# Attention scores on row halves inside column blocks, and a pair's probabilities side by side

## The chip, the cores and the metric

The kernel runs on one core of one Trainium2 chip. The metric is device time in microseconds for one execution of the whole program, lower is better. All numbers are fp32 in the inputs and the output.

## The reference

Two layers of an encoder trunk over 256 tokens of width 1024. Each layer is a SwiGLU half-step, a mixer, a second SwiGLU half-step and a gated input of a per-layer embedding. The change lies in the mixer, of which this is the outline:

```python
u = rmsnorm(x, g_mix[i]) @ w_in[i]                 # (256, 3072)
q, k, v, hy = jnp.split(u, [512, 1024, 1536], axis=-1)
y_na = neighbourhood_attention(q, k, v, na_rpb[i]) # 8 heads of 64
...                                                # short convolution of hy, split into x0, x1, hv
y_hy = x0 * long_conv(hv * x1, filt, hy_bias[i])   # 512 channels
y = jnp.concatenate([_rms(y_na), _rms(y_hy)], axis=-1) * g_out[i]
x = x + y @ w_out[i]
```

The attention's neighbourhood is a mask of the full 256 x 256 scores: per head s = q k^T / 8 + bias (a very negative number outside the neighbourhood), softmax over the keys, then the product with v.

## The kernel before

Activations are kept transposed: 128 channels on the partitions, 256 tokens along the free dimension. Matrix products are done in fp32r with every operand split in two parts, h (rounded) and l (the rest), and three products h·h, h·l, l·h; `mm3` is that. ScalarE makes h by a copy, VectorE makes l by a subtraction. Weights stream from HBM in pieces of 16 tiles on SP's queue and are split by ScalarE (L283) and VectorE (L285) in the same way.

The program is written as one order of matmuls, with everything else in "fibers", Python generators that issue a few instructions and then yield. A tick lets every live fiber take one step. `paced` counts the products that have been issued in units of 256 columns of an `mm3` and ticks once every three units, nine narrow matmuls. `fb.finish()` steps a fiber to its end, so that what it makes has been issued before the matmul that reads it. TensorE and ScalarE run in the order written; for the other engines the order is the framework's scheduler's. There are 8 PSUM banks, handed out by `bank()`, each 128 x 512 fp32.

The mixer runs through the list `ORDER`, token by token. `g0` to `g3`, `q0` to `q3`, `x0`, `x1` are column blocks: two products of 8 weight tiles each with the normed input, 48 narrow matmuls into the two halves of one bank (`columns`). A q block makes the queries and the keys of one pair of heads (128 channels: 64 of the even head, 64 of the odd one); class `QK` scales them by the norm (L728), and splits them: the keys whole (L733, L737), the queries into a zeroed tile of twice the width in which each head's 64 rows stand in a half of the columns of its own (L735, L739). `s` is the score block of a pair: for each head, two products of 128 queries with 256 keys, on all 128 rows, where the other head's rows are the zeros. `softmax` then works on one bank of a head: L762 and L764 on VectorE, L769 on ScalarE, a reciprocal L772, L776. `t` transposes the probabilities of a pair, 128 x 128 at a time (L783), one bank for each head, and splits them (L792, L794). `p` is `attend`: for each head and each half of the keys one `mm3` of v's 128 columns (the head's own 64 and 64 zeros) with that head's transposed probabilities, so that one 128 x 256 result holds both heads. `values` makes these zero-padded tiles of v: four memsets for each half of the tokens on POOL (L696, L697), a scaling L701, and copies and subtractions by quarters (L708, L712). `head_norm` scales the result (L802, L805) and adds up its squares, from which `Rstd` makes the norm of the attention's output: matmuls with ones (L415), a chain on VectorE (L388 to L432), a spread to all rows (L439).

`u` and `f` are the transposes and the forward transform of the long convolution, `i` its way back, `a` the projection of the attention's output, after which the other output's projection follows. The weights on the host are laid out in the order of the column blocks.

Of the kernel before, what the change touches and what calls it, by code (L numbers as in the profile page):

```python
# [79 lines left out]
def hybrid_trunk(ctx: ExitStack, tc: tile.TileContext, w, xT, pT, rpb, small, wf, zT, dft, idft, decay, out):  # L80
# [583 lines left out]
    def mixer(i):  # L664
# [25 lines left out]
        vh = [[t2(F32R, "vh") for _ in range(2)] for _ in range(2)]  # L690
        vl = [[t2(F32R, "vl") for _ in range(2)] for _ in range(2)]

        def values():
            for tt in range(2):
                for pp in range(2):
                    G.memset(f(vh[tt][pp]), 0.0)  # L696
                    G.memset(f(vl[tt][pp]), 0.0)  # L697
            yield from rs.wait()
            for tt in range(2):
                vf = t2()  # L700
                V.tensor_scalar(vf, vps[tt], rs.r[:, tt : tt + 1], None, op0=ALU.mult)  # L701
                yield
                for pp in range(2):
                    src = vf[:, pp * 256 : (pp + 1) * 256].rearrange("p (a b c) -> p a b c", a=2, b=2)
                    hv, lv = v2(vh[tt][pp]), v2(vl[tt][pp])
                    for par in range(2):
                        cs = slice(par * 192, par * 192 + 64)
                        S.copy(hv[:, :, cs], src[:, :, par])  # L708
                    yield
                    for par in range(2):  # L710
                        cs = slice(par * 192, par * 192 + 64)
                        V.tensor_sub(lv[:, :, cs], src[:, :, par], f(hv[:, :, cs]))  # L712

        class QK:


            def __init__(self, b):
                self.kh, self.kl = t1(F32R), t1(F32R)
                self.qh, self.ql = t2(F32R), t2(F32R)
                self.fb = spawn(self.go(b))  # L720

            def go(self, b):
                G.memset(f(self.qh), 0.0)
                G.memset(f(self.ql), 0.0)
                yield from rest(EV)
                yield from rs.wait()
                q = t2()
                V.tensor_tensor(v2(q), v2(b), rb2(), op=ALU.mult)  # L728
                yield
                where = [  # L730
                    (slice(64 * par, 64 * par + 64), slice(T * par, T * par + T)) for par in range(2)
                ]
                S.copy(self.kh, q[:, T:])  # L733
                for r, c in where:
                    S.copy(self.qh[r, c], q[r, :T])  # L735
                yield
                V.tensor_sub(self.kl, q[:, T:], f(self.kh))  # L737
                for r, c in where:
                    V.tensor_sub(self.ql[r, c], q[r, :T], f(self.qh[r, c]))  # L739

        class Head:
# [7 lines left out]
            def scores(self, st):  # L749
                st.fb.finish()  # L750
                b = bank()
                for tt in range(2):
                    qs = slice(T * self.par + tt * P, T * self.par + (tt + 1) * P)
                    mm3(b[:, tt * T : (tt + 1) * T], st.qh[:, qs], st.ql[:, qs], st.kh, st.kl, True, True)
                self.e = t2()
                self.fb = spawn(self.softmax(b), True)
# [21 lines left out]
            def turn(self):  # L778
                self.fb.finish()
                b = bank()  # L780
                for kt in range(2):
                    for tt in range(2):
                        PE.transpose(  # L783
                            b[:, kt * T + tt * P : kt * T + (tt + 1) * P],
                            self.e[:, tt * T + kt * P : tt * T + (kt + 1) * P],
                            ident,
                        )
                self.h, self.l = t2(F32R), t2(F32R)
                self.fb = spawn(self.parts(b), True)

            def parts(self, b):
                S.copy(self.h, b)  # L792
                yield
                V.tensor_sub(self.l, b, f(self.h))  # L794

# [11 lines left out]
        def attend(pair, hs):  # L807
            vfb.finish()
            ps = bank()[:, :T]
            n = 0  # L810
            for h in hs:
                h.fb.finish()
                for kt in range(2):
                    cs = slice((pair % 2) * 256 + h.par * P, (pair % 2) * 256 + (h.par + 1) * P)
                    ks = slice(kt * T, (kt + 1) * T)
                    a, b = vh[kt][pair // 2][:, cs], vl[kt][pair // 2][:, cs]
                    mm3(ps, a, b, h.h[:, ks], h.l[:, ks], n == 0, n == 3)
                    n += 1
            hl = t2(F32R, "y")
            yna.append((hl, spawn(head_norm(ps, nsq, pair, hl))))  # L820
# [41 lines left out]
        def turn(hs):  # L862
            for h in hs:
                h.turn()

        def scores(pair, st):
            hs = [Head(pair, par) for par in range(2)]
            for h in hs:
                h.scores(st)
            return hs  # L870
# [64 lines left out]
        def add(c, ps, st, e):  # L935
# [4 lines left out]
            e.tensor_add(x[c], x[c], t)  # L940
# [21 lines left out]
        qs, hs, added, wo = {}, {}, [], Tiles()  # L962
        for kind, j in MIXER:
            if kind == "g":
                gated(j, columns())
            elif kind == "q":
                qs[j] = QK(columns())
            elif kind == "x":
                outer(2 * j, columns())
            elif kind == "s":  # L970
                hs[j] = scores(j, qs.pop(j))
            elif kind == "t":
                turn(hs[j])
            elif kind == "p":
                attend(j, hs.pop(j))
                if len(yna) == 4:
                    na = Rstd(rna, nsq.parts, HY, [fb for _, fb in yna], STAT_NA, SPREAD_NA)
            elif kind == "u":
                u_turned()
            elif kind == "f":  # L980
                forward(j)
            elif kind == "i":
                backward(j)
                if len(yhy) == 4:
                    hy = Rstd(rhy, hsq.parts, HY, [fb for _, fb in yhy], STAT_HY, SPREAD_HY)
            elif kind == "a":
                added.append(spawn(add(j, project(wo, j, yna), na, V)))
        wo = Tiles()
        new_norm()
        for c in range(KD):  # L990
            ps = project(wo, c, yhy)

            def both(c=c, ps=ps):
                added[c].finish()
                yield from add(c, ps, hy, V)
# [165 lines left out]
def _weights(a):  # L1161
# [16 lines left out]
    for i in range(DEPTH):  # L1178
# [3 lines left out]
        for kind, j in MIXER:  # L1182
# [71 lines left out]
```

## Time and profile before

| | |
|---|---|
| time, median of 3 runs | 1093.13 us (1092.15 to 1093.78) |
| the profiled execution's own time | 1093.29 us |
| its span, first to last instruction | 1091.5 us |
| granted TensorE clock, mean | 0.994 |
| busy: PE, weight load, DVE, ACT, POOL | 1064.5, 964.0, 912.1, 649.4, 196.2 us |

PE is TensorE's matmuls, DVE VectorE, ACT ScalarE, POOL GpSimd; L12 is a line of the kernel. A matmul's duration runs to the modelled end of its result, so neighbouring matmuls overlap and a busy share near 100% doesn't by itself say how dense they are; the distance between two starts does. The mixers lie at about 213 to 329 us and 743 to 860 us of the span.

### The profile page before, as it was taken

To read this page: it belongs to the slowest core of one execution; us is meant where nothing else is said; L and a number is where in the kernel's file an instruction comes from. 1 tells how busy PE (TensorE), PEld (TensorE's weight loads), DVE (VectorE), ACT (ScalarE), POOL (GpSimd) and SP (SyncE) were. 2 spreads that over 40 slices of the span, in tenths; PEclk is the share of its full clock that TensorE was granted. 3 is DMA by queue.
4 is the path that set the end of the run, shared out by engine and by line. 5 is a ranking of instruction groups with operands and counts; after the bars stand their busy time and mean duration, and the time that the engine had idled before them with its cause. 6 is when DMAs were issued, how large, how long until landed. Compare 5 with 4: busy or idle time off the path is not lost.

```text
span 1091.5 us, 17975 instructions
## 1 busy us (share of the span) xinstructions
PE 1064.5 (98%) x6716; PEld 964.0 (88%) x6716; DVE 912.1 (84%) x1590; ACT 649.4 (59%) x1182; POOL 196.2 (18%) x232
## 2 busy tenths in 40 slices
PE   7989999999999999999999999999999999999995
PEld 6878888899997888888988888889999888888895
DVE  4999987898999988766789999788889999886564
ACT  7566665376736766544666665635765566665443
POOL 3111120411212211100111113023131311110101
PEclk9999999999999999999999999999999999999998
DMA  9566545554425655555465654555513465555621
GB/s 325 192 202 231 193 160 188 192 195 151 139 97 184 210 194 187 187 188 191 157 219 180 231 194 158 190 171 180 195 73 117 140 217 198 191 190 177 209 78 39
DMA packets 32983, 194.07 MB, mean 178 GB/s; under 512 B 3584, under 2 KB 6528, under 8 KB 10880
## 3 DMA queue, kind: packets, MB, share of 16 engines
q1 hardware_dynamic: 32896, 192.92, 51.6%
q8 instruction: 53, 0.87, 0.3%
q14 instruction: 34, 0.28, 0.1%
HBM read 191.86 MB, written 1.05 MB: 177 GB/s over the span
## 4 chain that ended last, share of the span: by engine, by line
PE 85%; DVE 10%; DMA 2%; ACT 2%; issue 1%; SPq 0%; ACTq 0%; DVEq 0%
PE ps L190 40%; PE ps L199 21%; PE ps L169 7%; PE ps L170 7%; PE ps L171 7%; DVE wl L285 3%; DMA raw<-in_w 2%; DVE x L940 1%; DVE s L939 1%; DVE rt L396 1%; DVE xg L367 1%; ACT wh L283 1%; PE ps L783 1%; DVE y L805 0%; PE ps L415 0%
## 5 line engine op out<-in xcount | busy, mean ns | idle before, releaser
L285 DVE TENSOR_TENSOR wl<-raw,wh 128x1024 fp32r<-128x1024 f32 (+1 forms) x350 | 427.6, 1244 | 98.4 <-PE ps L199 62.1
L283 ACT CAST wh<-raw 128x1024 fp32r<-128x1024 f32 (+1 forms) x350 | 362.1, 1041 | 156.8 <-PE ps L190 82.7
L190 PE MATMUL ps<-xg,wh 128*128 128x512 f32 x1408 | 346.7, 395 | 10.6 <-DVE xg L1088 6.5
L190 PEld LDWEIGHTS ps<-xg,wh 128*128 128x128 f32 x1408 | 259.3, 190 | 62.7 <-DVE xg L1088 7.2
L199 PEld LDWEIGHTS ps<-xg,wl 128*128 128x128 f32 x1408 | 182.4, 192 | 7.7
L199 PE MATMUL ps<-xg,wl 128*128 128x256 f32 x1408 | 184.6, 283 | 0.0
L190 PE MATMUL ps<-act,wh 128*128 128x512 f32 x704 | 173.0, 391 | 0.0
L190 PEld LDWEIGHTS ps<-act,wh 128*128 128x128 f32 x704 | 128.3, 189 | 23.8
L487 POOL TENSOR_TENSOR gu<-gu,rb 128x256 f32<-128x256 f32 x88 | 69.3, 792 | 393.1 <-DVE gu L207 324.6
L169 PE MATMUL ps<-xg,wh 128*128 128x256 f32 x448 | 127.5, 285 | 0.0
L171 PE MATMUL ps<-xg,wl 128*128 128x256 f32 x448 | 126.8, 283 | 0.0
L170 PE MATMUL ps<-xg,wh 128*128 128x256 f32 x448 | 126.7, 283 | 0.0
L353 POOL TENSOR_TENSOR acc<-acc,q 128x256 f32<-128x256 f32 x62 | 56.1, 905 | 328.9 <-ACT q L350 327.7
L199 PEld LDWEIGHTS ps<-act,wl 128*128 128x128 f32 x704 | 92.9, 191 | 5.1
L199 PE MATMUL ps<-act,wl 128*128 128x256 f32 x704 | 94.4, 282 | 0.0
L170 PEld LDWEIGHTS ps<-xg,wh 128*128 128x128 f32 x448 | 86.0, 192 | 0.1
L169 PEld LDWEIGHTS ps<-xg,wh 128*128 128x128 f32 x448 | 85.9, 192 | 0.1
L171 PEld LDWEIGHTS ps<-xg,wl 128*128 128x128 f32 x448 | 85.9, 192 | 0.0
L204 ACT COPY gu<-ps 128x256 f32<-128x256 f32 x176 | 56.1, 373 | 31.5 <-PE ps L199 31.2
L207 DVE TENSOR_TENSOR gu<-gu,ps 128x256 f32<-128x256 f32 x176 | 66.1, 411 | 0.0
L365 ACT ACTIVATE xg<-x,sm 128x256 fp32r<-128x256 f32 x56 | 28.1, 507 | 57.8 <-DVE x L524 40.4
L494 DVE TENSOR_TENSOR s<-s,gu 128x256 f32<-128x256 f32 x88 | 55.0, 634 | 0.4 <-ACT s L491 0.2
(194 smaller groups left out, 1298.7 us busy)
## 6 DMA issues: line engine op xcount, KB each, us to landing
raw<-in_w SPq DMA_DIRECT2D x172, 1024.0 KB, 4.9
bias<-in_rpb SPq DMA_DIRECT2D x16, 256.0 KB, 2.7
raw<-in_w SPq DMA_DIRECT2D x4, 256.0 KB, 4.8
x<-in_xT SPq DMA_DIRECT2D x8, 128.0 KB, 4.8
raw<-in_w SPq DMA_DIRECT2D x2, 512.0 KB, 5.3
t<-in_wf SPq DMA_DIRECT2D x4, 256.0 KB, 5.7
dec<-in_decay SPq DMA_DIRECT2D x4, 256.0 KB, 5.7
out<-o SPq DMA_DIRECT2D x4, 256.0 KB, 2.5
```

The lines of the kernel that those rows point to most:

```text
L169: PE.matmul(o, lh, rh, start=start, stop=False)
L170: PE.matmul(o, lh, rl, start=False, stop=False)
L171: PE.matmul(o, ll, rh, start=False, stop=stop)
L190: PE.matmul(b, lh, r, start=start, stop=False)
L199: PE.matmul(o, ll, rh, start=False, stop=stop)
L204: S.copy(dst, b[:, T:])
L207: V.tensor_add(dst, dst, b[:, :T])
L283: S.copy(h[:, a : a + k], src)
L285: V.tensor_sub(l[:, a : a + k], src, f(h[:, a : a + k]))
L353: G.tensor_add(self.ac, self.ac, q)
L487: G.tensor_mul(u, u, rb)
L494: V.tensor_mul(s, s, u)
```

## The change

- The queries are no longer set into a zeroed tile. `QK` scales the block, copies it whole (h) and subtracts whole (l), one 128 x 512 operation each; the two memsets of each pair on POOL go.
- A score block works on 64 rows at a time: the even head's on rows 0 to 63, the odd one's on rows 64 to 127, in turn, into two banks. The count of matmuls stays 12.
- `s0`, `s1` and `s2` are issued between the two halves of a column block (`q1+s0`: after the first product of q1), and the order of the other tokens changes.
- The transposes of a pair are ordered by the half of the keys, with both heads' probabilities side by side in one bank, so that they can be the 512 columns of one product.
- `attend` multiplies v's 128 columns of the pair, unpadded, by these 512 columns: 6 wide matmuls in place of 12 narrow ones. Of the 128 x 512 result two diagonal blocks are wanted; ScalarE copies them (2 copies of 64 x 256) into a tile in SBUF, one tick ahead of `head_norm`, which now reads that tile.
- `values` is one ScalarE scaling and one VectorE multiply-subtract for each half of the tokens, straight from PSUM; its memsets go.

```diff
-ORDER = "g0 q0 g1 s0 q1 g2 t0 s1 g3 q2 t1 p0 u0 q3 f0 s2 f1 p1 s3 t2 x0 x1 t3 i0 p2 p3 i1 i2 i3 a0 a1 a2 a3 a4 a5 a6 a7"
-MIXER = [(t[0], int(t[1])) for t in ORDER.split()]
+ORDER = "g0 q0 g1 q1+s0 g2 g3 t0 q2+s1 p0 u0 q3+s2 t1 f0 f1 p1 t2 s3 x0 x1 t3 i0 p2 p3 i1 i2 i3 a0 a1 a2 a3 a4 a5 a6 a7"
+MIXER = [[(t[0], int(t[1])) for t in b.split("+")] for b in ORDER.split()]
...
             for tt in range(2):
...
+                r = rs.r[:, tt : tt + 1]
+                S.activation(vh[tt], vps[tt], AF.Copy, scale=r)
+                yield
+                V.scalar_tensor_tensor(vl[tt], vps[tt], r, f(vh[tt]), op0=ALU.mult, op1=ALU.subtract)
+                yield
...
-                G.memset(f(self.qh), 0.0)
-                G.memset(f(self.ql), 0.0)
                 yield from rest(EV)
                 yield from rs.wait()
                 q = t2()
                 V.tensor_tensor(v2(q), v2(b), rb2(), op=ALU.mult)
                 yield
...
+                S.copy(self.h, q)
+                yield
+                V.tensor_sub(self.l, q, f(self.h))
...
+        def attend(pair, ps):
+
             vfb.finish()
...
+            b = bank()
+            for kt, (h, l, fb) in enumerate(ps):
+                fb.finish()
+                vs = slice(128 * pair, 128 * pair + 128)
+                mm3(b, vh[kt][:, vs], vl[kt][:, vs], h, l, kt == 0, kt == 1)
             hl = t2(F32R, "y")
-            yna.append((hl, spawn(head_norm(ps, nsq, pair, hl))))
+
+            def go():
+                y = t1(s="y")
+                for par in range(2):
+                    r = slice(64 * par, 64 * par + 64)
+                    S.copy(y[r], b[r, T * par : T * par + T])
+                yield
+                yield from head_norm(y, nsq, pair, hl)
+
+            yna.append((hl, spawn(go())))
...
         def turn(hs):
...
+            made = []
+            for kt in range(2):
+                b = bank()
+                for h in hs:
+                    h.fb.finish()
+                    for tt in range(2):
+                        o = T * h.par + tt * P
+                        PE.transpose(b[:, o : o + P], h.e[:, tt * T + kt * P : tt * T + (kt + 1) * P], ident)
+                h, l = t2(F32R), t2(F32R)
+
+                def go(b=b, h=h, l=l):
+                    split(b, h, l)
+                    yield
+
+                made.append((h, l, spawn(go(), True)))
+            return made
 
         def scores(pair, st):
             hs = [Head(pair, par) for par in range(2)]
-            for h in hs:
-                h.scores(st)
+            st.fb.finish()
+            banks = [bank(), bank()]
+            for tt in range(2):
+                qs = slice(tt * P, (tt + 1) * P)
+                for n, (a, b) in enumerate(((st.h, st.h), (st.h, st.l), (st.l, st.h))):
+                    for par, o in enumerate(banks):
+                        r = slice(64 * par, 64 * par + 64)
+                        PE.matmul(o[:, tt * T : (tt + 1) * T], a[r, qs], b[r, T:], start=n == 0, stop=n == 2)
+                    paced()
+            for h, o in zip(hs, banks):
+                h.scored(o)
             return hs
...
+        for block, *inner in MIXER:
+            emit(*block, (lambda: emit(*inner[0])) if inner else None)
```

More of the change, by code (lines that the diff above doesn't have):

```diff
@@ L747, in __init__, with scored @@
                 nc.sync.dma_start(self.bias, rpb[i, 2 * pair + par])
[L749 to L754, printed above, removed]
+            def scored(self, b):
                 self.e = t2()
@@ L776, in softmax @@
                     S.activation(e[:, cs], e[:, cs], AF.Copy, scale=ri[:, tt : tt + 1])
[L778 to L794, printed above, removed]
         yna, yhy = [], []
@@ L961, in mixer, with emit @@
         vfb = spawn(values())
-        qs, hs, added, wo = {}, {}, [], Tiles()
-        for kind, j in MIXER:
+        qs, hs, ps, added, wo = {}, {}, {}, [], Tiles()
+        stats = {}
+        def emit(kind, j, between=None):
             if kind == "g":
-                gated(j, columns())
+                gated(j, columns(between))
             elif kind == "q":
-                qs[j] = QK(columns())
+                qs[j] = QK(columns(between))
             elif kind == "x":
-                outer(2 * j, columns())
+                outer(2 * j, columns(between))
             elif kind == "s":
@@ L972, in mixer @@
             elif kind == "t":
-                turn(hs[j])
+                ps[j] = turn(hs.pop(j))
             elif kind == "p":
-                attend(j, hs.pop(j))
+                attend(j, ps.pop(j))
                 if len(yna) == 4:
-                    na = Rstd(rna, nsq.parts, HY, [fb for _, fb in yna], STAT_NA, SPREAD_NA)
+                    stats["na"] = Rstd(rna, nsq.parts, HY, [fb for _, fb in yna], STAT_NA, SPREAD_NA)
             elif kind == "u":
@@ L1181, in _weights @@
         put(win[8:12].transpose(1, 0, 2, 3))
-        for kind, j in MIXER:
+        for (kind, j), *_ in MIXER:
             if kind in "gqx":
```

55 lines of the change are left out of this document (8 added, 47 removed).

## The prediction

> **What bounds the kernel now.** I read the page first, then busy time by stretch, then the chain of waits inside the mixer, then the order of matmuls there. The page:
>
> ```profile
> PE 1064.5 (98%) x6716; PEld 964.0 (88%) x6716; DVE 912.1 (84%) x1590; ACT 649.4 (59%) x1182; POOL 196.2 (18%) x232
> PE 85%; DVE 10%; DMA 2%; ACT 2%; issue 1%; SPq 0%; ACTq 0%; DVEq 0%
> ```
>
> TensorE is busy for 98% of the span and holds 85% of the chain that ended last, so a change is worth what it takes out of TensorE's row of matmuls, or out of the holes in it. This one touches only the mixer, which runs twice. The first run by stretches (start:end, length, busy time of PE, PEld, DVE, ACT, POOL, then clock, DMA share, GB/s):
>
> ```profile
> 213.00:247.00 34.00, 34.00 (x270) 33.28 (x269) 30.60 (x64) 23.45 (x46) 4.96 (x8) 1.00 0.61 207
> 247.00:282.00 35.00, 34.86 (x269) 33.34 (x267) 30.90 (x54) 22.58 (x52) 8.70 (x11) 1.00 0.43 146
> 282.00:303.00 21.00, 21.00 (x179) 21.00 (x178) 19.81 (x35) 15.92 (x36) 3.02 (x4) 1.00 0.39 126
> 303.00:336.00 33.00, 31.48 (x241) 30.06 (x240) 32.26 (x83) 16.25 (x31) 6.03 (x7) 1.00 0.40 136
> ```
>
> Up to 303 us TensorE is full, at clock 1.00, and VectorE has 7.5 us to spare between 213 and 282. From 303 us it turns round: VectorE is busy 32.26 of 33 us and TensorE has holes. The chain of waits names the place where it changes hands (the sums of squares of the attention's output, L415, and the VectorE work behind them):
>
> ```profile
> 293.67 0.87 PE ps L783 x8
> 302.81 0.35 PE ps L415 x4
> 303.38 0.65 DVE rt L388
> ```
>
> What TensorE gains ahead of 302.8 us therefore counts in full, if VectorE is no later at that place than now. The attention lies ahead of it. Its matmuls, from the timeline of TensorE; durations overlap, so the price of one is the step from its start to the next start:
>
> ```profile
> 205.89 0.39 PE L169 MATMUL ps<-wh,xg 128*128 128x512 f32 x1
> ...
> 213.14 0.39 PE L171 MATMUL ps<-wh,xg 128*128 128x512 f32 x1
> 261.58 1.04 PE L783 MATMUL ps<-ident,t 128*128 128x128 f32 x8
> 262.37 0.36 PE L169 MATMUL ps<-t,vh 128*128 128x256 f32 x1
> 262.57 0.28 PE L170 MATMUL ps<-t,vh 128*128 128x256 f32 x1
> 278.96 0.28 PE L169 MATMUL ps<-s,t 128*128 128x256 f32 x1
> ...
> 280.28 0.28 PE L171 MATMUL ps<-s,t 128*128 128x256 f32 x1
> 280.42 1.74 PE L783 MATMUL ps<-ident,t 128*128 128x128 f32 x8
> 281.92 0.36 PE L169 MATMUL ps<-xg,wh 128*128 128x256 f32 x1
> ```
>
> Wide matmuls (512 columns): 32 steps in 7.25 us, 0.227 each. Narrow ones (256): 11 steps in 1.32 us, 0.120 each. Eight transposes (128 columns) and the matmul behind them take 0.99 us; less one narrow step that is 0.87, or 0.109 each. Half the columns save only a tenth of the step, so something besides the moving data, I take it the weight load, holds a step near 0.11.
>
> **The change part by part.** *Scores.* Now each pair of heads has 12 narrow matmuls on 128 rows, half of them zeros:
>
> ```profile
> L169 PE MATMUL ps<-s,t 128*128 128x256 f32 x32 | 9.2, 288 | 0.0
> ```
>
> Three such lines make 96 matmuls, at 0.120 us 11.5 us over both layers. Afterwards there are also 96, but each on 64 rows, upper and lower half in turn, into two banks. No row here has a 64-row matmul. Best end: the halves run side by side and a couple costs one narrow step, 48 x 0.120 = 5.8 us, gain 5.8. Other end: they go one behind the other, held by the weight load at the transposes' 0.109, 96 x 0.109 = 10.5, gain 1.0. I take the first, because the two halves share neither rows nor a bank, which is where these two kinds of matmul differ from all that the trace shows in a row. [...]
>
> *Changes of array height.* Each of the 8 score blocks goes from 128 rows to 64 and back, 16 changes, six of the eight in the middle of a column block. Nearest rows: at 262.37 the matmul starts 0.03 us behind the last transpose and the next 0.20 later, together two usual steps, so that change of mode costs 0. Upper end: the tail of a matmul, 0.28 less 0.12 = 0.16, 16 x 0.16 = 2.6 us. Neither row changes the height; I take the middle, 1.3 us lost. [...]
>
> *Attend.* 96 narrow matmuls become 48 wide ones, half of whose output is thrown away: 96 x 0.120 = 11.5 against 48 x 0.227 = 10.9, gain 0.6 us; between 0.5 and 0.7 by the rounding of the steps.
>
> *Transposes.* 64 before and after. What goes is the wait at the third pair's (t2): the order now has only f1, p1 and s3 between s2 and t2. The block at 280.42 takes 1.50 to the next matmul, that at 261.58 takes 0.79, so 0.71. In the second layer:
>
> ```profile
> 792.35 1.03 PE L783 MATMUL ps<-ident,t 128*128 128x128 f32 x8
> 811.04 0.28 PE L171 MATMUL ps<-s,t 128*128 128x256 f32 x1
> 811.44 1.91 PE L783 MATMUL ps<-ident,t 128*128 128x128 f32 x8
> 813.11 0.36 PE L169 MATMUL ps<-xg,wh 128*128 128x256 f32 x1
> ```
>
> 1.67 less 0.79, and 0.28 ahead of it: 1.16. Together 1.9 us. Afterwards half of q3, t1, f0, f1 and p1 (2.9 + 0.9 + 2 x 2.7 + 1.4 = 10.6 us by the steps) stand between, so I take the whole 1.9 as gained; the other end is 0. Late next is the second of the new orders:
>
> *A shorter way for the third pair's split.* Score block s2 now stands in the middle of q3, after p0 (1.4), u0 (0.9) and half of q3 (2.9): 5.1 us behind the end of q2. What waits is the split of q2 into two parts, three steps VectorE, ScalarE, VectorE:
>
> ```profile
> 262.84 0.68 DVE L728 TENSOR_TENSOR t<-ps,rb 128x512 f32<-128x512 f32 x1
> 263.44 1.28 DVE L794 TENSOR_TENSOR t<-ps,t 128x512 fp32r<-128x512 f32 x2
> 267.60 0.86 DVE L739 TENSOR_TENSOR t<-t,t 64x256 fp32r<-64x256 f32 x2
> 801.29 0.86 DVE L739 TENSOR_TENSOR t<-t,t 64x256 fp32r<-64x256 f32 x2
> ```
>
> q2's matmuls end at 261.58 and 792.35 (the transposes' start), the split at 268.46 and 802.15: 6.9 and 9.8 us. Now that is hidden by blocks in between; then it is not. Unshortened it would hold TensorE for 1.8 + 4.7 = 6.5 us, with the half block of q3 and all behind it queued there. It gets shorter: t1's part of VectorE (1.28) goes behind it, and the last step becomes one whole-width operation, 0.68 for 1.25 (0.42 for the keys' half and 0.86), saving 0.57. That leaves 5.05 and 7.95 against 5.1, so 0 and 2.85; I take 2.0 lost in all, between 0 and 6.5. s0, s1 and s3 have at least 8.6 us of matmuls ahead of them, more than three of these four numbers, and I cost them at nothing.
>
> *The other engines.*
>
> ```profile
> L701 DVE TENSOR_SCALAR t<-ps,rt 128x512 f32<-128x512 f32 x4 | 3.0, 744 | 0.0
> L712 DVE TENSOR_TENSOR vl<-t,vh 128x128 fp32r<-128x128 f32 x16 | 4.2, 282 | 0.0
> L739 DVE TENSOR_TENSOR t<-t,t 64x256 fp32r<-64x256 f32 x16 | 6.7, 417 | 0.3
> L762 DVE SCALAR_TENSOR_TENSOR t<-ps,bias 128x512 f32<-128x512 f32 x16 | 10.5, 681 | 0.1
> L805 DVE SCALAR_TENSOR_TENSOR y<-s,sm,y 128x256 fp32r<-128x256 f32 x8 | 6.2, 788 | 0.0
> L805 DVE SCALAR_TENSOR_TENSOR y<-ps,sm,y 128x256 fp32r<-128x256 f32 x8 | 3.8, 475 | 0.8 <-ACT q L350 0.8
> L204 ACT COPY gu<-ps 128x256 f32<-128x256 f32 x176 | 56.1, 373 | 31.5 <-PE ps L199 31.2
> L696 POOL MEMSET vh<- 128x512 f32 x8 | 4.2, 526 | 0.0
> ```
>
> VectorE gives up 7.5 us of value splitting (L701, L712) for four operations of 0.68, 2.7 us, and 8 x 0.57 = 4.6 of query splitting: 9.4 us less; against it eight L805 read y from SBUF, up to 0.31 dearer each, 2.5. Net 6.9 us less over two layers, nearly all ahead of 302.8, more than TensorE is to gain there, so VectorE does not get later. ScalarE gets 16 copies of 64 rows (at most 0.37 each, 6.0 us) and loses as much in merged casts; it has idle time in every stretch. POOL loses 32 memsets of 0.53, hidden now. DMA: the same bytes, in another order.
>
> One wait is added: the copy of y takes one more turn of the scheduler (nine narrow steps, 1.1 us) between p3 and the sums of L415, where the chain changes hands. VectorE has other work queued there (the backward products), so I take half, 1.1 us lost over two layers, between 0 and 2.2.
>
> **The sum**, against the profiled execution's 1093.29 us (span 1091.5; the median of the runs is 1093.13, 0.16 below): -5.8 + 1.3 - 0.6 - 1.9 + 2.0 + 1.1 = -3.9, 1089.4 us.
>
> **The rivals.** *Weight loads stay in a row.* For it: the transposes' 0.109. The scores gain 1.0 in place of 5.8: 1094.2, about no change. [...]
>
> *Each change of half costs like a change of height* (slower). Place: between every two score matmuls. At 0.08 (half of the tail's 0.16) on top of 0.12, 96 x 0.20 = 19.2, a loss of 7.7 in place of the gain of 5.8: 1102.9. It decides from 0.003 per change on, where the whole is 2.2 us (0.2%) slower. Against it: the halves share no rows.
>
> *The gain stands, but s2's wait takes its full 6.5*: 1093.9, no change. For it: the second layer's 9.8 us.
>
> **How the numbers follow.** Forecast 0.60, weight loads 0.24, changes of half 0.07, full wait 0.09. A measurement here tells about 0.2%, 2.2 us. The forecast's own range adds its terms' ends: 1085.0 (no drain, no waits) to 1091.8 (drain and added wait in full); of its 0.60, 0.09 lies above 1090.9. The loads' rival, 1090.5 to 1096, is "same" for two thirds and "slower" for 0.06. So faster 0.52, same 0.34, slower 0.14. The range 1085.5 to 1095.5 leaves out the changes of half and a few hundredths at both ends.
>
> **What would show it.** Right: in a score block two 64-row matmuls start within 0.02 us of each other and a block of twelve takes about 0.75 us; attend steps at 0.227; no wait at t2; a hole of at most 2.9 us in front of s2's second couple; L415 of the attention about 2 us earlier against the mixer's start, and VectorE's chain behind it as long as now. Wrong: twelve steps of 0.11 or more in a score block, a hole at s2 above 3 us a layer, or TensorE waiting longer at the end of the mixer, where VectorE is the bound.

## The result and the profile after

The changed kernel takes 1100.73 us (1099.21 to 1103.19) against 1093.07 us (1092.15 to 1093.78): a ratio of 1.0072, 95% interval 1.0057 to 1.0087. It is 7.7 us slower, where 3.9 us faster was forecast, and outside the range. The profiled execution shown here took 1101.27 us, 0.5 above the median. The page:

```profile
span 1099.2 us, 17764 instructions
PE 1064.5 (97%) x6668; PEld 959.4 (87%) x6668; DVE 907.5 (83%) x1558; ACT 651.4 (59%) x1170; POOL 180.6 (16%) x200
PE 79%; DVE 12%; ACT 5%; DMA 2%; issue 1%; SPq 0%; ACTq 0%; DVEq 0%
```

TensorE has 48 matmuls less and the same busy time, and its share of the chain that ended last fell from 85 to 79%, while ScalarE's rose from 2 to 5%: TensorE now waits for short chains on the two other engines. Busy time by stretch, after, then before; in each the four rows are, for each layer, the mixer's first matmul (the wide ones that make v) to the first projection, and from there to the first matmul of the next half-step (columns as in the prediction):

```profile
207.34:307.42 100.08, 96.91 (x720) 91.36 (x719) 82.97 (x141) 65.48 (x130) 15.72 (x14) 0.98 0.45 157
307.42:335.59 28.17, 25.23 (x206) 24.50 (x204) 26.83 (x76) 12.49 (x23) 3.08 (x4) 1.00 0.33 113
742.86:841.98 99.12, 95.59 (x720) 89.87 (x719) 83.64 (x139) 64.40 (x128) 17.27 (x14) 1.00 0.41 142
841.98:870.15 28.17, 25.26 (x207) 24.53 (x205) 26.83 (x76) 12.50 (x23) 3.06 (x4) 1.00 0.33 113
```

```profile
205.89:303.45 97.56, 97.42 (x747) 93.97 (x746) 86.06 (x159) 66.17 (x138) 23.27 (x31) 1.00 0.47 162
303.45:329.56 26.11, 24.59 (x203) 24.04 (x201) 25.59 (x73) 11.48 (x22) 2.35 (x3) 1.00 0.35 122
736.67:834.64 97.97, 97.69 (x748) 93.95 (x746) 85.79 (x160) 64.37 (x134) 23.93 (x30) 1.00 0.44 147
834.64:860.72 26.08, 24.59 (x202) 24.03 (x200) 25.52 (x70) 12.70 (x25) 2.92 (x3) 1.00 0.35 122
```

The attention's stretch was to get shorter; it got 2.5 and 1.2 us longer, with PE busy 0.5 to 2.1 us less inside it: holes. The stretch behind it got 2.1 us longer in both layers, and VectorE is busy for 26.8 of its 28.2 us. VectorE did lose work up to the first projection (3.1 and 2.2 us, where 6.9 in all had been forecast); it didn't help, because what TensorE waits for are single steps in a chain.

*A score block.* The timeline of TensorE, after; the last column is the count of a group:

```profile
239.00 0.28 PE L172 MATMUL ps<-xg,wl 128*128 128x256 f32 x1
239.21 0.39 PE L851 MATMUL ps<-t 64*128 64x256 f32 x2
239.43 0.40 PE L851 MATMUL ps<-t,t 64*128 64x256 f32 x4
239.66 0.28 PE L851 MATMUL ps<-t 64*128 64x256 f32 x2
239.78 0.40 PE L851 MATMUL ps<-t,t 64*128 64x256 f32 x4
240.11 0.39 PE L170 MATMUL ps<-xg,wh 128*128 128x256 f32 x1
240.34 0.28 PE L171 MATMUL ps<-xg,wh 128*128 128x256 f32 x1
```

The four groups of 2, 4, 2 and 4 are the twelve matmuls. Two start together (0.003 us apart) and couples follow each other at 0.115 us (239.43 to 239.66 is two couples): the halves do run side by side. But the first couple takes 0.22 (239.21 to 239.43), the last one 0.21 (from about 239.90 to 240.11), and the matmuls next to the block 0.21 and 0.22 in place of 0.12. From 239.00 to 240.34 less two narrow steps the block takes 1.10 us; 0.72 had been forecast without the changes of height, and 1.44 is the old price.

*The wait at s2*, with, in brackets, the idle time before the instruction and what ended it:

```profile
267.42 0.28 PE L172 MATMUL ps<-xg,wl 128*128 128x256 f32 x1
268.98 0.39 PE L851 MATMUL ps<-t 64*128 64x256 f32 x2 [1.28 <-ACT t L716]
270.02 0.50 PE L851 MATMUL ps<-t,t 64*128 64x256 f32 x4 [0.65 <-DVE t L718]
804.45 0.38 PE L851 MATMUL ps<-t 64*128 64x256 f32 x2 [1.23 <-ACT t L716]
805.49 0.50 PE L851 MATMUL ps<-t,t 64*128 64x256 f32 x4 [0.66 <-DVE t L718]
```

By the starts, less the usual step, it costs 1.44 + 0.97 = 2.41 us in the first layer and 2.36 in the second. First the copy (h) is late, then the subtraction (l). VectorE's timeline in the first layer shows what stands ahead of them:

```profile
260.38 1.28 DVE L736 SCALAR_TENSOR_TENSOR t<-ps,bias 128x512 f32<-128x512 f32 x2
261.58 1.27 DVE L738 TENSOR_REDUCE mx<-t 128x2 f32<-128x512 f32 x2
266.75 0.68 DVE L714 TENSOR_TENSOR t<-ps,rb 128x512 f32<-128x512 f32 x1
269.28 0.68 DVE L718 TENSOR_TENSOR t<-t,t 128x512 fp32r<-128x512 f32 x1
```

q2's matmuls end at 262.32. The scaling (L714) comes 4.4 us later, behind the softmax of pair 1 (L736, L738: s1 now lies inside q2), a split of weights and the split of u (L212). On ScalarE the copy L716 (268.33) then stands behind the `head_norm` of p0. The subtraction ends at 269.96.

*A stretch at half clock behind it.* Two windows: the first begins half a microsecond after the block in the first layer, the second lies behind the same wait in the second layer:

```profile
271.30:274.70 3.40, 3.40 (x19) 3.40 (x18) 3.21 (x5) 0.18 (x1) 0.00 (x0) 0.50 0.92 366
805.50:808.90 3.40, 3.40 (x32) 3.27 (x33) 2.53 (x5) 1.44 (x3) 0.00 (x0) 1.00 0.81 294
```

For 3.4 us the granted clock is 0.50 and a narrow step 0.213 in place of 0.120, about 1.5 us lost. The same wait in the second layer was followed by none (last row), so a wait of this size does not bring one each time.

*A new wait in i0 and one at the end of the mixer.*

```profile
298.63 0.28 PE L171 MATMUL ps<-idft_l,t 128*128 128x256 f32 x1
300.14 0.39 PE L172 MATMUL ps<-idft_h,t 128*128 128x256 f32 x1 [1.24 <-DVE t L894]
333.54 0.28 PE L172 MATMUL ps<-y,wl 128*128 128x256 f32 x1
335.59 1.19 PE L191 MATMUL ps<-xg,wh 128*128 128x512 f32 x3 [1.78 <-DVE xg L368]
```

```profile
298.27 1.22 DVE L286 TENSOR_TENSOR wl<-raw,wh 128x1024 fp32r<-128x1024 f32 x1
299.40 0.69 DVE L894 TENSOR_TENSOR t<-t,t 128x512 fp32r<-128x512 f32 x1
```

In i0 the last low part of the spectrum (L894, VectorE's timeline) stands behind a split of weights; the matmul for it is 1.40 us late (0.57 + 1.40 in the second layer). No such wait was there before. From the start of the last projection's matmul to the next half-step it is now 2.05 us, in both layers, against 1.30 and 0.93 (328.26 to 329.56 and 859.79 to 860.72). Before, on TensorE's timeline:

```profile
329.56 0.98 PE L190 MATMUL ps<-xg,wh 128*128 128x512 f32 x3 [1.01 <-DVE xg L367]
860.72 0.74 PE L190 MATMUL ps<-xg,wh 128*128 128x512 f32 x2 [0.66 <-DVE xg L367]
```

The attention's sums of squares, which the prediction had about 2 us earlier against the mixer's start, come later: at 101.2 and 100.2 us behind it (308.50 less 207.34, 843.06 less 742.86) against 96.8 in both layers before, and now behind the first projection instead of ahead of it.

*The books.* For both mixers, up to 200 matmuls into the half-step behind each, from the starts of all matmuls; a hole is a step less the usual step of its kind (0.227, 0.120, 0.109, and 0.060 for a 64-row one):

| | predicted, us | measured, us |
|---|---|---|
| matmul work: 155.14 to 151.95 a layer | -6.4 | -6.4 |
| changes of height, 8 x 0.38 | +1.3 | +3.0 |
| t2's wait | -1.9 | -1.6 |
| s2's wait, 2.41 + 2.36 | +2.0 | +4.8 |
| i0's wait, 1.40 + 1.97 | not seen | +3.4 |
| end of the mixer: spread of the second norm +0.9, two steps behind its sums +0.6, start of the half-step +1.9 | +1.1 | +3.4 |
| half-step's waits for weights, shorter | not seen | -2.2 |
| two stretches at half clock (271.3, 336.2) | not seen | +3.0 |
| other | | -0.4 |
| sum | -3.9 | +7.0 |

The second stretch at half clock, at 336.2, costs less than its share of the 3.0 in that table. With it, 200 matmuls from the half-step's start take 36.35 us in the first layer, without it 35.86 in the second: the waits for weights there (0.35 and 0.50 us in the second layer) are gone beside it, and about 0.5 us stays.

Outside the mixers +0.7: 0.57 in a later half-step, 1.45 ahead of the first mixer (both kernels have half clock near 70 us, 0.75 over 69.4 to 76.2 before, 0.54 after), and -1.3 at the end, where before had 0.53 from 1080.8 to 1084.2.

### The profile page after: what moved, and what is told of

Read it like the earlier page. It is cut to its first block, busy times and chain, and to the rows that moved or that the text cites. A ratio compares the mean times of both kernels' runs of the same rounds, so it can differ in the third digit from the quotient of the medians.

```text
span 1099.2 us, 17764 instructions
## 1 busy us (share of the span) xinstructions
PE 1064.5 (97%) x6668; PEld 959.4 (87%) x6668; DVE 907.5 (83%) x1558; ACT 651.4 (59%) x1170; POOL 180.6 (16%) x200
## 4 chain that ended last, share of the span: by engine, by line
PE 79%; DVE 12%; ACT 5%; DMA 2%; issue 1%; SPq 0%; ACTq 0%; DVEq 0%
PE ps L191 40%; PE ps L200 21%; PE ps L170 6%; PE ps L172 5%; PE ps L171 5%; DVE wl L286 3%; ACT wh L284 2%; DMA raw<-in_w 2%; DVE xg L368 1%; DVE x L925 1%; DVE y L761 1%; DVE rt L397 1%; DVE s L924 1%; PE ps L851 0%; ACT t L211 0%
## 5 line engine op out<-in xcount | busy, mean ns | idle before, releaser
L191 PE MATMUL ps<-xg,wh 128*128 128x512 f32 x1408 | 348.1, 396 | 10.9 <-DVE xg L1078 6.3
L354 POOL TENSOR_TENSOR acc<-acc,q 128x256 f32<-128x256 f32 x62 | 53.1, 857 | 331.7 <-ACT q L351 330.4
```

Source lines behind the costliest of these rows:

```text
L191: PE.matmul(b, lh, r, start=start, stop=False)
L354: G.tensor_add(self.ac, self.ac, q)
```

## The experiments

The questions: is it the order, one of the parts, or the scheduler's turns; and do the holes account for the time. In the tables the ratio is to the kernel before.

**First: four edits of the changed kernel.**

`e1_old_order`: the order of before, no block inside another.

```diff
-ORDER = "g0 q0 g1 q1+s0 g2 g3 t0 q2+s1 p0 u0 q3+s2 t1 f0 f1 p1 t2 s3 x0 x1 ...
+ORDER = "g0 q0 g1 s0 q1 g2 t0 s1 g3 q2 t1 p0 u0 q3 f0 s2 f1 p1 s3 t2 x0 x1 ...
```

> The changed kernel with the order of tokens of the kernel before; everything else of the change stays. Theory A (three places): the loss of 7.7 us is made of TensorE's wait in front of s2 (about 2.3 us a layer, and a stretch of half clock behind it in the first layer), of a new wait in i0 for the last spectral part (1.4 and 2.0 us), and of the changes of array height (about 0.5 us a score block). The first two come from the order, so they go here (8 to 9.5 us) and t2's wait comes back (about 1.9): 1092 to 1096. Theory B (the end of the mixer): VectorE is the bound from the sums of squares of the attention's output on, and these come later by the copy of y and its extra turn; whatever the order gains or loses ahead of it is paid back there: 1098 to 1101, with TensorE waiting longer in the projections.

`e2_s2_late`: s2 behind t1, t2 between x0 and x1.

```diff
+ORDER = "... q3 t1 s2 f0 f1 p1 s3 x0 t2 x1 t3 i0 ...
```

> The changed kernel with s2 taken out of the middle of q3 and put behind t1, s3 ahead of x0 and t2 between x0 and x1. Theory A: the wait in front of s2 goes, 4.6 us and up to 1.5 of half clock, nothing comes in its place at t2 or t3; i0's wait stays at 1.4 to 2.0 us a layer: 1094 to 1097. Theory B: no change by more than 1.5 us, 1099 to 1102.

`e3_spectral_sooner`: three turns less in the fiber that multiplies the spectrum (one ahead of the loop, one in each of its two rounds), so that L894 is issued sooner.

```diff
-            yield
             for m, (k0, k1_) in ((a, (kre, kim)), (2 + a, (kim, kre))):
...
                 yield
-                yield
```

> The changed kernel with three of the scheduler's turns taken out of the fiber of the spectral products, so that its last split is issued three turns earlier. Theory A: the wait in i0 goes, 3.4 us, the wait in front of s2 stays: 1096 to 1098. Theory B: no change by more than 1.5 us.

`e4_halves_in_turn`: in a score block all six matmuls of the upper half, then the six of the lower.

```diff
-                    for par, o in enumerate(banks):
+            for par, o in enumerate(banks):
+                r = slice(64 * par, 64 * par + 64)
+                for tt in range(2):
...
+                    if tt:
+                        paced(3)
```

> The changed kernel with the twelve matmuls of a score block issued all for the upper rows, then all for the lower ones, in place of in turn; nothing else differs. If the halves overlap only when they alternate, a block's steps go from 0.057 us in the mean to 0.11 to 0.12: 8 x 0.7 = 5 to 6 us slower than the changed kernel, 1105 to 1107, on top of the same waits. If the 64-row matmul is quicker in itself, the steps stay near 0.06 and the time near 1100.

| | us | ratio, 95% |
|---|---|---|
| e1_old_order | 1100.36 | 1.0067 [1.0052, 1.0082] |
| e2_s2_late | 1100.62 | 1.0073 [1.0056, 1.0090] |
| e3_spectral_sooner | 1099.19 | 1.0052 [1.0036, 1.0068] |
| e4_halves_in_turn | 1101.37 | 1.0078 [1.0058, 1.0098] |

Each wait went where its edit took it from, and the times followed little. Those of e1 and e2 lie in theory B's ranges, e3's gain of 1.5 us at the edge of it, and none in theory A's. In all three the stretch from the first projection on is 1.6 to 2.1 us a layer longer than before, as theory B has it; the rest, 0.5 to 2.1 us a layer, is lost ahead of it, in waits and half clock. With the old order s2's wait is gone and t2's is back, larger than before (2.69 us and three times 0.29 in the first layer, 2.70 in the second), with half clock behind it at 284.1 and 816.6, and a third stretch at 335.3. In e2 the waits are at t3 (0.45 and three times 0.29) and in i0 (0.77 + 1.49), with half clock at 332.9, 831.3 and 868.8. In e3 i0's wait (3.4 us) is gone, s2's stays, and three stretches at half clock (270.7, 803.2, 868.0) in place of two took a part of the gain back. So the order alone is not the cause. e4's block, on TensorE's timeline:

```profile
237.99 0.28 PE L172 MATMUL ps<-xg,wl 128*128 128x256 f32 x1
238.20 0.38 PE L851 MATMUL ps<-t 64*128 64x256 f32 x1
238.42 0.39 PE L851 MATMUL ps<-t,t 64*128 64x256 f32 x2
238.55 0.39 PE L851 MATMUL ps<-t 64*128 64x256 f32 x2
238.77 0.40 PE L851 MATMUL ps<-t,t 64*128 64x256 f32 x4
...
239.45 0.39 PE L170 MATMUL ps<-xg,wh 128*128 128x256 f32 x1
239.68 0.28 PE L171 MATMUL ps<-xg,wh 128*128 128x256 f32 x1
```

1.69 less two steps is 1.45 us, against 1.10 in turn. The edit took only a part of the overlap away: the single starts (the group at 238.55 is the lower half's first and the upper half's fourth) show the lower half's first three matmuls beginning within 0.01 us of the upper half's third, fifth and sixth, so that the twelve have nine starts in place of six. A 64-row matmul with no partner takes 0.110 to 0.120 us to the next start, as long as a padded one: it is not quicker in itself, and the gain is the overlap. Twelve without any would take 12 x 0.120 and the 0.38 of the two changes of height, an estimated 1.82 us. The difference between the two orders is 8 x 0.35 = 2.8 us, half of what was expected. The time rose by 0.6 only, which by itself would have spoken for the other theory: the two mixers are 1.6 us longer, with one stretch of half clock in them (805.1) in place of two, and the first one starts 1.0 us sooner (206.33 against 207.34).

**Second: the ends and the parts.**

`e5_norm_sooner`: without the added turn ahead of `head_norm`, and the attention's sums one turn sooner.

```diff
-STAT_NA = 1
+STAT_NA = 0
...
                     S.copy(y[r], b[r, T * par : T * par + T])
-                yield
```

> The changed kernel with two of the scheduler's turns taken away between the last attend and the sums of squares (the turn behind the copy of y, and the turn that the attention's norm rests). The first experiments showed the end of the mixer about 1.65 us a layer longer than before in every version with the copy of y. If that is the added turn, it goes: 3 to 4 us quicker than the changed kernel, 1096 to 1098, with the sums of squares about where they were before against the first projection. If VectorE's work there is what got longer, nothing changes: 1099 to 1101.

`e6_three_waits`: e5 and e3, and `QK` without its pause ahead of the scaling.

```diff
             def go(self, b):
-                yield from rest(EV)
                 yield from rs.wait()
```

> The changed kernel with the turns of the norm (as in e5_norm_sooner), the three turns of the spectral products (as in e3_spectral_sooner) and one turn of the split of queries and keys taken away, so that each of the four waits found on TensorE starts sooner. If the waits and the half-clock windows behind them are the whole loss, it comes to the kernel before or below it: 1088 to 1093. If they only move to other places, it stays over 1095.

`e7_halves_only`: the kernel before, with its order, `turn`, `attend` and `values`, but with `QK` and the score blocks of the change, at 4 units of pace a block as before.

```diff
+                    for par, o in enumerate(banks):
+                        r = slice(64 * par, 64 * par + 64)
+                        PE.matmul(o[:, tt * T : (tt + 1) * T], a[r, qs], b[r, T:], start=n == 0, stop=n == 2)
+                    if n:
+                        paced()
```

> The kernel before with the score blocks on row halves alone (queries and keys split whole, no zeroed tiles, two banks in turn), with its own order, its own padded values, transposes and attend, and as many turns a score block as before. By the steps measured in the changed kernel a block costs 12 x 0.06 + 0.5 for the two changes of height against 12 x 0.12: 0.2 less, 8 times, 1.8 us, and t2's wait of 1.9 may grow, as both heads' softmax now start together: 1090.5 to 1094. If it is over 1095, the row halves themselves carry the loss.

`e8_attend_only`: the kernel before with `values`, `turn` and `attend` of the change, its added turn too.

```diff
+                mm3(b, vh[kt][:, vs], vl[kt][:, vs], h, l, kt == 0, kt == 1)
...
+                    S.copy(y[r], b[r, T * par : T * par + T])
+                yield
+                yield from head_norm(y, nsq, pair, hl)
```

> The kernel before with the unpadded values, the side by side transposes and the wide attend with its copy of y, but its own order and its own zero-padded score blocks on 128 rows. By the steps 0.6 us less on TensorE; by the turn that the copy of y adds, 3 to 3.5 us more at the ends of the two mixers: 1094 to 1097. If the added turn is not what costs there, 1091 to 1093.5.

| | us | ratio, 95% |
|---|---|---|
| e5_norm_sooner | 1104.93 | 1.0109 [1.0094, 1.0124] |
| e6_three_waits | 1091.98 | 0.9991 [0.9982, 1.0001] |
| e7_halves_only | 1090.59 | 0.9980 [0.9971, 0.9989] |
| e8_attend_only | 1096.15 | 1.0027 [1.0016, 1.0038] |

e5 missed its aim: from the first projection to the half-step it got 2.4 us shorter in both layers (25.75 and 25.74), but TensorE now stood at the sums ahead of it (1.38 and 1.27), s2's wait grew (2.73 and 2.67), and half clock came at 270.2, 300.9 and 836.8. e6, which shortens three chains at once, has no half clock in the first mixer, one in the second (834.5), and is level with before; 8.7 us separate it from the changed kernel, and all that differs is a few turns. The longest wait that it still has in the mixers is at the sums of squares:

```profile
302.00 0.61 PE L416 MATMUL ps<-onesf,nacc 128*128 128x1 f32 x4 [1.81 <-POOL nacc L354]
```

The half clock in its second mixer cost nothing that shows: it falls into the projections, the wait for the next half-step behind them shrinks from 1.89 to 0.41 us, and the two mixers take 159.80 and 159.79 us, up to the 200th matmul behind.

The parts: the halves alone gain 2.5 us, the attend part alone loses 3.1. e7's attention stretch is 1.00 and 1.18 us shorter than before, and its end of the mixer has not got worse (26.34 and 26.08 against 26.11 and 26.08):

```profile
205.57:302.13 96.56, 96.03 (x747) 91.28 (x746) 83.59 (x151) 63.82 (x130) 18.59 (x23) 1.00 0.48 164
302.13:328.47 26.34, 24.58 (x203) 24.03 (x201) 25.62 (x73) 11.49 (x22) 2.32 (x3) 1.00 0.36 121
735.58:832.37 96.79, 96.18 (x748) 91.28 (x746) 83.06 (x152) 62.22 (x126) 20.22 (x22) 1.00 0.44 148
832.37:858.45 26.08, 24.57 (x202) 24.02 (x200) 25.52 (x70) 12.71 (x25) 2.92 (x3) 1.00 0.36 122
```

**Third: what makes the attend part dear, and whether the parts add up.**

`e9_attend_no_turn`: e8 without the added turn.

```diff
                     S.copy(y[r], b[r, T * par : T * par + T])
-                yield
                 yield from head_norm(y, nsq, pair, hl)
```

> e8_attend_only (1096.15 us) with one edit: the turn between the copy of y and the norm's work is taken away, so that the copy, the scaling and the square are issued in one step; the rest before the sums stays. If the added turn is what e8 loses at the ends of the mixers, it comes back to 1092 to 1093.5. If it is the copies on ScalarE, or VectorE reading y from SBUF, it stays at 1095 to 1097.

`e10_halves_t2_later`: e7 with t2 between x0 and x1 (`... s3 x0 t2 x1 t3 ...`) and e3's three turns less.

> e7_halves_only (1090.6 us) with t2 moved from behind s3 to between x0 and x1, and the spectral fiber's three turns taken away as in e3_spectral_sooner (t2's forced turns, which now fall away, had advanced it). t2's wait of about 1.2 us a layer goes and nothing takes its place: 1087.5 to 1089.5. If the wait only moves on to t3 or i0: 1090 to 1092.

`e11_halves_and_attend`: e7 and e9 together: all of the change but its order, its pace and its added turn.

> The whole change except its order and its added turn: row halves, unpadded values, side by side transposes, wide attend, in the order of the kernel before and with as many turns a score block. If the changed kernel's loss is order and turns alone, the parts add up: e7's 1090.6 less 0.6 for attend, 1089.5 to 1091. If the parts disturb each other (both heads' softmax needed for each transposed bank, in front of t2), t2's wait grows and it stays at 1092 to 1095.

`e12_halves_attend_t2_later`: e11 with t2 between x0 and x1.

> e11_halves_and_attend with t2 between x0 and x1 and the spectral fiber three turns sooner, as in e10_halves_t2_later. If t2's wait is all that e11 still loses in the middle: 1086.5 to 1089. If waits move on to t3 or i0: 1090 to 1092.

| | us | ratio, 95% |
|---|---|---|
| e9_attend_no_turn | 1093.49 | 1.0010 [1.0002, 1.0019] |
| e10_halves_t2_later | 1090.40 | 0.9977 [0.9969, 0.9986] |
| e11_halves_and_attend | 1095.07 | 1.0018 [1.0009, 1.0027] |
| e12_halves_attend_t2_later | 1094.34 | 1.0012 [1.0003, 1.0020] |

The turn: 1096.15 less 1093.49 is 2.7 us, for one turn a pair. It lies where the prediction put it. From the first projection to the next half-step, e8 and then e9:

```profile
305.32:333.24 27.92, 25.27 (x207) 24.51 (x205) 26.58 (x75) 12.42 (x24) 2.69 (x4) 1.00 0.33 112
837.83:866.10 28.27, 26.53 (x207) 26.10 (x205) 27.03 (x76) 13.59 (x27) 3.16 (x4) 0.94 0.33 113
306.45:332.13 25.68, 24.58 (x203) 24.02 (x201) 25.15 (x73) 11.60 (x22) 1.97 (x3) 1.00 0.37 123
837.60:863.69 26.09, 24.63 (x203) 24.03 (x201) 25.50 (x70) 12.82 (x25) 2.92 (x3) 1.00 0.35 122
```

2.2 us longer in each layer with the turn, 4.4 together, and half clock in the second (0.94). The stretches ahead of the first projection are 1.7 us shorter with it (97.95 and 97.84 against 99.16 and 98.35) and the first 200 matmuls of the half-steps behind 1.1, which leaves 1.6 in these two profiles for the 2.7 between the medians. (The profiled execution of e9 was 2.8 us above its median; these stretches are not where it lost them.)

The parts do not add up: -2.5 and +0.4 give -2.1, e11 is +2.0. Its t2 is where: the first bank holds both heads side by side, so its four transposes need all four of ScalarE's scalings (L749: two heads, two halves of the queries), where before the second head's were hidden behind the first head's other transposes. The timeline and the clock of e11:

```profile
279.98 1.96 PE L830 MATMUL ps<-ident,t 128*128 128x128 f32 x8 [1.18 <-ACT t L749]
```

```profile
278.60:282.00 3.40, 2.00 (x14) 1.24 (x11) 3.22 (x6) 3.34 (x9) 2.53 (x4) 1.00 0.00 0
282.00:285.40 3.40, 3.40 (x18) 3.40 (x17) 3.40 (x7) 3.40 (x10) 0.83 (x1) 0.51 0.43 154
814.50:817.90 3.40, 3.40 (x18) 3.40 (x17) 3.40 (x7) 3.40 (x11) 0.69 (x1) 0.50 0.00 0
```

The wait is 1.40 us, and then each of the next three transposes is 0.29 late, 2.27 in all, against 0.6 and 1.0 before, and in both layers a stretch at half clock follows. Moving t2 (e10, e12) takes that wait away, but only moves it: to the product of the values with the low part of the probabilities (1.33 and 0.94 in e10; 1.48 and 0.53 in e12), and in e12 to the sums too (L415, 2.03 and 1.44), with half clock at 304.4.

**Fourth: the pace, the half clock, and another order.**

`e13_four_units`: the changed kernel, with 4 units of pace for a score block as before, not 6.

```diff
-                    paced()
+                    if n:
+                        paced()
```

> The changed kernel with 4 units of the scheduler's pace a score block, as before, in place of 6; all else as changed. If the units shift the turns that the waits and the mixer's end hang on (the first matmuls behind the mixer waited 2.06 us in every version with 6 units, 1.29 and 0.93 in those with 4; and a stretch of 0.57 us elsewhere appears with 6 only): 2 to 4 us quicker, 1096.5 to 1099. If not: 1100 to 1102.

`e14_four_units_no_turn`: e13 without the added turn; against e11 it differs in the order alone.

> e13_four_units with the turn behind the copy of y taken away too. If turns are all that parts the changed kernel from e11_halves_and_attend (1095.1), and the new order is worth nothing either way: 1094 to 1097. If the new order costs of itself: 1098 or more.

`e15_filled_wait`: e11, with twelve narrow matmuls into a spare bank ahead of t2's transposes, whose result nobody reads.

```diff
+                if j == 2:
+                    idle = bank()
+                    for _ in range(12):
+                        PE.matmul(idle[:, :T], ones, dft_h[:, 0], start=True, stop=True)
```

> e11_halves_and_attend (1095.1 us) with 12 matmuls of 256 columns into a spare bank, read by nobody, ahead of t2's transposes, where TensorE waits 1.4 us and then three times 0.29. The extra 1.44 us of work fits into the first wait. If the half-clock stretches behind this wait (seen in both mixers of e11's profile) come from TensorE's idleness, they go and the time falls by 2 to 3.5 us, to 1091.5 to 1093, though there is more work. If the clock drops for another reason: 1095 or more.

`e16_halves_s2_first`: e7 with s2 ahead of f0 and f1 (`... q3 s2 f0 f1 p1 s3 t2 ...`) and e3's three turns less.

> e7_halves_only (1090.6) with s2 issued ahead of f0 in place of between f0 and f1, so that f0 too lies between it and t2, and the spectral fiber's three turns taken away. t2's wait, 1.2 us a layer in e7, goes: 1087.5 to 1089.5. If the softmax then only competes with the spectral products on VectorE and the wait shows at i0 or p2: 1090 to 1091.5.

| | us | ratio, 95% |
|---|---|---|
| e13_four_units | 1097.79 | 1.0042 [1.0029, 1.0055] |
| e14_four_units_no_turn | 1098.66 | 1.0051 [1.0037, 1.0064] |
| e15_filled_wait | 1092.73 | 0.9995 [0.9987, 1.0004] |
| e16_halves_s2_first | 1089.12 | 0.9963 [0.9951, 0.9975] |

e13: the two extra units a block are worth 2.9 us, on balance of waits that go and come. At 4 units the start of the half-step is back to 1.29 and 0.93 us and the 0.57 us in the later half-step is gone. e14: without the turn nothing is gained (1098.66 against 1097.79): the end of the mixer is about as short as before, but s2 and i0 wait 8.0 us in both layers together, where e11's t2 waits 4.5; both have two stretches at half clock, and the difference of 3.5 is about that of the times (3.6). So in this kernel the new order exchanges t2's wait for a larger one, and the turn's 2.7 us (e8 against e9) is its price in the old order alone.

e15 tests where the half clock comes from. The same two windows as in e11:

```profile
282.00:285.40 3.40, 3.33 (x28) 3.16 (x28) 3.40 (x6) 3.38 (x8) 1.90 (x2) 1.00 0.43 149
814.50:817.90 3.40, 3.40 (x31) 3.40 (x30) 3.40 (x6) 3.40 (x11) 0.23 (x1) 1.00 0.02 5
```

TensorE does 1.44 us more work in each layer and the kernel is 2.3 us faster, with the clock at 1.00 through both mixers. So in e11 it was TensorE's idleness that brought the half clock: data that comes no sooner costs less when the wait is filled. The stretches here are 3.4 us long at clock 0.50, and waits of 1.9 to 3.6 us in all, with matmuls between their parts, were enough. Over the 18 profiles, the mixers and the starts of the half-steps have 36 places with waits of 1.9 us or more in all within a few microseconds; 24 of them are followed by a stretch, and no stretch follows less.

e16 is the fastest of all: 4.1 us faster than before, at the upper end of what was expected. In the first layer no wait is left at s2 or t2, in the second 1.02 us and twice 0.29 at t2.

## Why the prediction was wrong

- *Halves overlap*: right. 0.057 to 0.058 us a matmul against the 0.060 assumed; e4 shows that a 64-row matmul is no quicker in itself (0.110 to 0.120 with no partner). That the weight load holds a lone step near 0.11 was the author's estimate from the transposes' 0.109, and no run shows its cause. The rivals of loads in a row and of a price for each change of half are refuted.
- *Changes of array height*: right kind, wrong size. 0.38 us a block, 3.0 in all, against 1.3, and above the upper end of 2.6: the tail of a matmul was counted once for each change, but on both sides of a change the neighbouring step is long too (0.21 to 0.22 us each, in place of 0.12). No run shows the drain that the forecast's own range names at its two ends; what the runs show are these long steps, 0.38 us a block.
- *Attend*: right, 0.229 a wide matmul, 0.6 us.
- *t2's wait goes*: right, 1.6 of 1.9. But its forced finishes had been two turns of the scheduler for everything else; without them the spectrum's fiber, which needs 14 turns, had exactly 14 and no spare, and its last step slid behind a split of weights: 3.4 us at i0, which the prediction put at nothing. That this is why i0 waits is argued from the count of the kernel's yields; that a few turns less end the wait is shown by e3.
- *s2's wait*: right in kind, wrong in size: 4.8 against 2.0, inside the bounds of 0 to 6.5. From q2's last matmul to the end of its split it takes 7.6 us in both layers, where the prediction had 5.05 and 7.95. t1's part of VectorE did go behind it, but the new order put s1's softmax in front of it (2.55 us of L736 and L738, by the timeline above), and that was not counted.
- *The added turn*: 2.7 in the old order (e8 against e9), above the bound of 2.2. The half of it that VectorE's other work was to hide was not hidden: VectorE is busy for 26.8 of the 28.2 us there. In the new order its price is not shown, since taking it away gained nothing (e14) or, with the sums a turn sooner, lost 4.2 us (e5).
- *The pace of a score block*, 6 units for 4: a part of the change that was not costed at all. 2.9 us (e13), of which 1.9 is the wait for the half-step and 0.6 the later half-step.
- *The clock*: taken as 1.00, since the mixers showed 1.00. New waits of 1.9 and 2.4 us brought two stretches, which cost about 1.5 us at s2 and 0.5 at the half-step.

The step that failed is the sum of the waits. Between -3.9 and +7.0 lie 10.9 us; 8.5 of them are waits of TensorE that were sized too low or put at nothing (s2 2.8, i0 3.4, the end of the mixer 2.3). The matmul work, -6.4, came out as forecast. The sum took each wait as a term of its own, at the place where it was seen, and VectorE's spare 7 us as cover for all. The runs show the holes as what one chain of VectorE and ScalarE steps leaves behind TensorE: a wait that went mostly let the next step be late in its place (e1, e2, e10, e12), though not always (e6, e16).

What stays open: why a wait of the same size brings half clock in one layer and not in the other, and what fixes the number of such stretches near 70 us and the clock at 1080 us. With one stretch near 70 us the first mixer starts at 205.7 us, with two at 206.7 (medians over the 18 profiles); what follows the 200th matmul behind the second mixer takes 193.1 to 194.5.

## What to carry to other kernels

In a kernel with a hand-written order, count the turns: a forced finish that goes, a unit of pace that comes, a turn ahead of the step that bounds a stretch are terms of the sum. Here they were worth up to 2.9 us each, against 0.6 for the wide products, and the price of one depends on what waits around it. Take a change apart before it is judged: of this one the row halves were worth keeping (-2.5 us, with a better order -4.1), the other part and the order were not. Waits of TensorE of 1.9 to 3.6 us in all were followed in 24 of 36 places by 3.4 us at half clock, which cost 1.5 us where TensorE's matmuls set the pace and 0 to 0.5 where it would have waited anyway. Filling the wait with 1.44 us of matmuls took both of e11's stretches away (e15).

## What the runs showed of the hardware

- Two 64-row matmuls on different row halves and banks started 0.003 us apart and cost together one narrow step of 0.115 us (the changed kernel). With no partner one took 0.110 to 0.120 (e4). With all six of one half issued first, three of the other half's still began beside them (e4). Changing between 128 and 64 rows and back cost 0.38 us a block (1.10 against 0.72, the changed kernel).
- Stretches of 3.4 us at clock 0.50 followed 24 of 36 waits of 1.9 to 3.6 us within an otherwise full stream of matmuls, and none shorter; with e11's wait filled, its two were gone (e15).
